# The forgetting heads' bias taken as the row of running sums, in four causal strips per head

## The chip, the cores and the metric

One core of one Trainium2 chip runs the whole program. The metric is device time in microseconds (us), the median of the runs shown. The engines are named as in the profile: PE (TensorE, the matrix engine; PEld is its loading of weights), DVE (VectorE), ACT (ScalarE), POOL (GpSimd) and SP (SyncE, which here only issues transfers). Each engine works through its own instructions strictly in order.

## The reference, cut to what matters

The program is one decoder layer on a sequence of 512 positions with width 1024: a feed-forward half step, a mixing step with two branches of attention, and a second feed-forward half step. The change lies in branch A, the forgetting attention, with 8 heads of 64:

```python
cum = jnp.cumsum(log_f, axis=1).transpose(0, 2, 1)
for start in range(0, S, Q_BLOCK):            # blocks of 128 queries
    end = start + Q_BLOCK
    logits = jnp.einsum('bqhd,bkhd->bhqk', q[:, start:end], k[:, :end]) * scale
    logits = logits + cum[:, :, start:end, None] - cum[:, :, None, :end]
    logits = jnp.where(kpos <= qpos, logits, NEG_INF)
    p = jax.nn.softmax(logits, axis=-1)
    outs.append(jnp.einsum('bhqk,bkhd->bqhd', p, v[:, :end]))
```

The first summand of the bias, `cum` at the query, is one number for a whole row of the softmax, and a softmax does not change when a constant is added to its row. The second, `cum` at the key, differs from column to column. Branch B, the sparse attention, has 8 more heads with a bias by distance and a selection of the 128 best keys.

## The kernel before, in words

Matmuls are made in three passes of a split number (high times high, low times high, high times low; lines 155 to 157). The feed-forward steps come first and last. Between them, from about 350 to 650 us, lie the projections and the 16 heads of attention: heads 0 to 7 are the forgetting ones, 8 to 15 the sparse ones. The order of PE is written out by hand: each head has four steps s = 0 to 3, and step s computes the scores of query block i = 3 - s (`ps_qk`, line 929 its last matmul) against n = 128 (i + 1) keys. Between the steps stand pieces of the projections, by a table of amounts (`FILL`), which keep PE busy while the other engines make the softmax. On PE the scores of one head are followed a head later by the transposes of its probabilities (`pt`, line 1251) and, one step after these, by the products with the values (`po`, lines 1261 and 1262).

In this stretch the order on DVE, ACT, POOL and SP is set when the program is built, by a scheduler that places each instruction where it expects its inputs to be ready; on the chip the order is fixed. The names that matter:

- `softmax_block` (lines 1233 to 1245). DVE adds bias and scores and takes the minimum of the row (scores stand there with reversed sign; line 1240, `p<-ps_qk,b`, called the score sum below), ACT takes the exponential (`p<-p,mn`, 1242), DVE the reciprocal of the row's sum (`rs`, 1243), and POOL multiplies by it (`p<-p,rs`, 1244).
- `flip` copies the transposed probabilities into a high part on ACT (`ph`, 1255) and a low part on DVE (`pl`, 1256).
- `get_bias(g)` (1306) loads, one head ahead, for a forgetting head the 512 running sums of that head into all 128 partitions (`cb`, 256 KB, from `cum_rows` in DRAM). Then for each of the four blocks POOL makes a tile `b`: it adds the negative running sum of the query (`ncum`, line 1314), and writes the large number BIG above the diagonal into the last 128 columns (line 1315).
- `forget` (1147) makes the running sums `cum` in the stretch before the heads, and from them `ncum` on DVE (line 1176), and writes `cum_rows`.
- Other work of POOL here: the inverse root for the norm of queries and keys (`rh`, 900), that norm's product (`kn`, 1004), and the sum of two halves of a head's result (`o`, 1272). Other work of DVE: the low parts of the weights (`wl`, 150), of the heads' results (`oAl`, 1276), of keys (`kl`, 890) and queries (`st`, 920), and until about 456 us the selection of keys for branch B (`m` and `sc`, 1189 to 1194).
- SP issues the loads of weights (line 143, three buffers `ra`, `rb`, `rc` in turn), the bias loads (1308) and copies of key halves (1302), in one queue.

Of the kernel before, what the change touches and what calls it, by code (L numbers as in the profile page):

```python
# [12 lines left out]
F32 = mybir.dt.float32  # L13
F32R = mybir.dt.float32r
AF = mybir.ActivationFunctionType
OP = mybir.AluOpType
# [3 lines left out]
P = 128  # L20
T = 512
NT = T // P
# [14 lines left out]
H = 8  # L37
# [3 lines left out]
BIG = 1e30  # L41
S_W = 208
# [13 lines left out]
def tile_hybrid_layer(ctx: ExitStack, tc: tile.TileContext, a: dict):  # L56
    nc = tc.nc
# [727 lines left out]
    with tc.tile_pool(name="begin", bufs=1) as bp, tc.manual_schedule(  # L785
# [40 lines left out]
        for nm in ("w_gate1", "w_up1"):  # L826
            tag = next(raw_tags)
# [41 lines left out]
    with (tc.tile_pool(name="mix", bufs=1) as mp, ExitStack() as att_ctx,  # L869
# [3 lines left out]
        rt = rb = None  # L873
        tn, fv, iq, pA, ga, gb = {}, {}, [], [], [], []
        kept = mp_dram.tile([P, 5, T], F32, name="kept")
        sg = at.tile([P, NT, S_W - 128], F32, name="sg")
        sd = [at.tile([P, NT, 2, DH], F32, tag="cb", bufs=2, name="sd") for _ in range(2)]
        dkh = at.tile([P, T], F32R, name="dkh")
        dkl = at.tile([P, T], F32R, name="dkl")
        dvv = at.tile([P, NT, P], F32R, name="dvv")  # L880
        cum = at.tile([P, NT, H], F32, name="cum")
        ncum = at.tile([P, NT, H], F32, name="ncum")
        dram = att_ctx.enter_context(tc.tile_pool(name="dram", bufs=1, space=bass.MemoryType.DRAM))
        cum_rows = dram.tile([H, T], F32, name="cum_rows")
        wi = at.tile([P, NT, H], F32, name="wi")
# [261 lines left out]
        def forget():  # L1147

            z = small.tile([P, NT, H], F32, tag="z", bufs=1, name="z")
            V.tensor_add(z, sg[:, :, 64:72], bf[:, None, :].to_broadcast([P, NT, H]))  # L1150
            na = small.tile([P, NT, H], F32, tag="na", bufs=1, name="na")
            V.scalar_tensor_tensor(na, z, -1.0, z, op0=OP.mult, op1=OP.min)
            e = small.tile([P, NT, H], F32, tag="e", bufs=1, name="e")
            S.activation(e, na, AF.Exp)
            u1 = small.tile([P, NT, H], F32, tag="u1", bufs=1, name="u1")
            V.tensor_scalar(u1, e, 1.0, None, op0=OP.add)
            ln = small.tile([P, NT, H], F32, tag="ln", bufs=1, name="ln")
            S.activation(ln, u1, AF.Ln)
            cr = small.tile([P, NT, H], F32, tag="cr", bufs=1, name="cr")
            V.tensor_scalar(cr, u1, 1.0, None, op0=OP.subtract)  # L1160
            V.tensor_sub(cr, e, cr)
            V.reciprocal(u1, u1)
            V.tensor_mul(cr, cr, u1)
            V.tensor_add(ln, ln, cr)
            lf = small.tile([P, NT, H], F32, tag="lf", bufs=1, name="lf")
            V.scalar_tensor_tensor(lf, z, 0.0, ln, op0=OP.min, op1=OP.subtract)
            before = small.tile([P, NT, H], F32, tag="u1", bufs=1, name="before")
            G.memset(before[:, 0], 0.0)
            for t in range(1, NT):
                V.tensor_add(before[:, t], before[:, t - 1], lf[:, t - 1])  # L1170
            yield
            pc = psum.tile([P, T], F32, tag="pt", bufs=2, name="pc")
            PE.matmul(pc[:, :NT * H], trin, lf.rearrange("p t h -> p (t h)"), start=True, stop=False)
            PE.matmul(pc[:, :NT * H], ones, before.rearrange("p t h -> p (t h)"), start=False, stop=True)
            V.tensor_copy(cum, pc[:, :NT * H].rearrange("p (t h) -> p t h", t=NT))
            V.tensor_scalar(ncum, cum, -1.0, None, op0=OP.mult)
            yield
            ps = psum.tile([P, T], F32, tag="pt", bufs=2, name="ps_ct")
            for t in range(NT):
                PE.transpose(ps[0:H, t * P:(t + 1) * P], cum[:, t], ident)  # L1180
            cum_t = tmp_tile("cum_t")[0:H]
            S.copy(cum_t, ps[0:H])
            nc.sync.dma_start(cum_rows, cum_t)
# [104 lines left out]
        def get_k(g):  # L1288
# [14 lines left out]
                out.append(k)  # L1303
            return out

        def get_bias(g):
            cb = at.tile([P, T], F32, tag="cb", bufs=2, name="cb")
            nc.sync.dma_start(cb, cum_rows[g:g + 1, :].to_broadcast([P, T]) if g < H else a["rel"][g - H])

            def bias(i):  # L1310
                n = P * (i + 1)
                b = tmp_tile("b")
                if g < H:
                    G.tensor_scalar(b[:, :n], cb[:, :n], 1.0, ncum[:, i, g:g + 1], op0=OP.mult, op1=OP.add)
                    G.affine_select(out=b[:, i * P:n], in_=b[:, i * P:n], compare_op=OP.is_ge, fill=BIG, base=0,
                                    pattern=[[-1, P]], channel_multiplier=1)
                else:
                    G.tensor_sub(b[:, :n], sc[i] if i else cpos, cb[:, T - n:T])
                return b[:, :n]
            return bias  # L1320

# [5 lines left out]
        for step in range(30):  # L1327
# [6 lines left out]
            if step == 15:  # L1334
                nq = get_q(0)
            if step == 24:
                nb = get_bias(0)
        prod.finish(upto["fv0"])


# [33 lines left out]
            return upto["dq1"] if g < 6 else upto["ga7"] if 4 * g + s < 4 * 9 + 2 else len(units)  # L1374

        for g in range(2 * H):
            q, k, bias = nq, nk, nb
            probs[g] = [None] * NT
            st = [small.tile([P, NT], F32, tag=nm, name=nm) for nm in ("mn", "rs")]
            for s in range(NT):  # L1380
# [4 lines left out]
                softmax_block(g, NT - 1 - s, q, k, bias, probs[g], st)  # L1385
                prod.run(FILL[g] / 2, limit(g, s))
                if g + 1 < 2 * H:
                    if s == 0:
                        nb = get_bias(g + 1)
                    if s == 0 and g % 2:  # L1390
                        nk = get_k(g + 1)
                    if s == 1 and g % 2:
                        nq = get_q(g + 1)
# [131 lines left out]
```

## Time and profile before

| | |
|---|---|
| median of 3 runs | 1044.01 us (1043.91 to 1044.5) |
| the profiled execution | 1043.44 us, its span 1041.7 us |
| PE busy in the span | 1027.9 us (99%) |
| DVE, ACT, POOL busy | 851.7, 668.8, 256.6 us |
| the forgetting heads' stretch, 420 to 532 us: PE, DVE, ACT, POOL busy | 105.35, 92.87, 78.35, 78.13 of 112 us |
| granted clock of PE | 1.00 throughout |

The page's parts follow each other: busy times, the span in 40 slices, transfers by queue, the chain of work that ended last, the costliest groups of instructions, and the transfers. The span is the time from the first to the last instruction that was profiled; the time of an execution contains about 2 us around it. In a row of a timeline the first number is the start in us from the span's start, the second the duration; a bracket gives the idle time of the engine before it and what ended it. PE's matmuls overlap, so that its busy time contains no gap that is shorter than one of them.

### The profile page before, as it was taken

The page shows a single profiled execution, that of the slowest core. Times are in us where ns is not written, and L with a number is a line of the kernel's source. Part 1 is how long each engine was busy: PE and PEld are TensorE (multiplying, and loading weights), DVE is VectorE, ACT ScalarE, POOL GpSimd, SP SyncE. Part 2 cuts the span into 40 slices and gives each one's busy share as a digit, 9 for nine tenths or more (in the row PEclk, how much of TensorE's full clock was granted, in tenths as well). Part 3 has the DMA queues.
Part 4 walks back from the last instruction along what each step waited for, and adds up shares of the span by engine and source line. Part 5 has one row for each costly group of instructions (what it writes and reads, how often), then busy time and mean ns, then how long its engine had stood idle before and what let it go on. Part 6 is the DMA issues. An engine that isn't in the chain of part 4 may idle for free.

```text
span 1041.7 us, 19489 instructions
## 1 busy us (share of the span) xinstructions
PE 1027.9 (99%) x7424; PEld 960.6 (92%) x7424; DVE 851.7 (82%) x1405; ACT 668.8 (64%) x1118; POOL 256.6 (25%) x324
## 2 busy tenths in 40 slices
PE   9999999999999999999999999999999999999998
PEld 8889999999999999989887788888889999999998
DVE  6897888897989779977868765853987888988887
ACT  6547765865787765567767665433736865875783
POOL 1100111120121124285867552000100210111111
PEclk9999999999999999999999999999999999999999
DMA  7444755666567367633314311532553665567554
GB/s 257 108 152 120 158 161 132 150 163 175 124 142 185 113 166 190 182 97 93 86 57 132 119 54 52 181 112 81 131 164 96 146 150 177 129 162 192 131 128 132
DMA packets 57341, 142.66 MB, mean 137 GB/s; under 512 B 6424, under 2 KB 15768, under 8 KB 57248
## 3 DMA queue, kind: packets, MB, share of 16 engines
q1 hardware_dynamic: 39600, 110.21, 34.1%
q0 software_dynamic: 17504, 30.94, 16.6%
q8 instruction: 58, 0.95, 0.4%
q10 hardware_dynamic: 144, 0.27, 0.1%
q14 instruction: 35, 0.29, 0.1%
HBM read 104.94 MB, written 3.42 MB: 104 GB/s over the span
## 4 chain that ended last, share of the span: by engine, by line
PE 89%; DVE 5%; POOL 3%; issue 2%; DMA 1%; ACT 1%; POOLq 0%; DVEq 0%; ACTq 0%
PE pB L155 5%; PE pB L157 5%; PE pB L156 5%; PE ps_f L155 3%; PE pA L155 3%; PE pA L157 3%; PE pA L156 3%; PE ps_f L157 3%; PE ps_f L156 3%; PE dB L157 2%; PE dB L155 2%; PE dB L156 2%; PE ps_t L157 2%; PE ps_t L155 2%; PE ps_t L156 2%; PE dA L156 2%
## 5 line engine op out<-in xcount | busy, mean ns | idle before, releaser
L123 ACT CAST wh<-s 128x1024 fp32r<-128x1024 f32 (+1 forms) x90 | 86.8, 965 | 66.8 <-PE pC L156 31.5
L130 DVE TENSOR_TENSOR wl<-s,wh 128x1024 fp32r<-128x1024 f32 (+1 forms) x90 | 100.4, 1116 | 19.9 <-ACT wh L123 19.9
L155 PE MATMUL ps_t<-wh,xh 128*128 128x256 f32 (+1 forms) x288 | 81.2, 282 | 0.0
L157 PE MATMUL ps_t<-wh,xl 128*128 128x256 f32 (+1 forms) x288 | 80.4, 279 | 0.0
L156 PE MATMUL ps_t<-wl,xh 128*128 128x256 f32 (+1 forms) x288 | 80.3, 279 | 0.0
L155 PE MATMUL pB<-tbh,wh 128*128 128x256 f32 x288 | 79.5, 276 | 0.0
L156 PE MATMUL pB<-tbl,wh 128*128 128x256 f32 x288 | 79.5, 276 | 0.0
L157 PE MATMUL pB<-tbh,wl 128*128 128x256 f32 x288 | 79.5, 276 | 0.0
L249 POOL DMA_DIRECT2D b<-gu x12 | 10.4, 864 | 220.3 <-DVE rb L449 89.4
L155 PE MATMUL ps_f<-xh,wh 128*128 128x512 f32 (+1 forms) x152 | 59.0, 388 | 0.0
L157 PE MATMUL ps_f<-xh,wl 128*128 128x512 f32 (+1 forms) x152 | 57.9, 381 | 0.0
L156 PE MATMUL ps_f<-xl,wh 128*128 128x512 f32 (+1 forms) x152 | 57.7, 380 | 0.0
L1242 ACT ACTIVATE p<-p,mn 128x512 f32<-128x512 f32 (+1 forms) x64 | 36.1, 564 | 29.5 <-DVE mn L1240 29.2
L155 PEld LDWEIGHTS ps_t<-wh,xh 128*128 128x128 f32 x288 | 54.5, 189 | 0.5
L156 PEld LDWEIGHTS ps_t<-wl,xh 128*128 128x128 f32 x288 | 54.4, 189 | 0.5
L157 PEld LDWEIGHTS ps_t<-wh,xl 128*128 128x128 f32 x288 | 54.4, 189 | 0.2 <-DVE xl L168 0.2
L157 PEld LDWEIGHTS pB<-tbh,wl 128*128 128x128 f32 x288 | 54.1, 188 | 0.0
L156 PEld LDWEIGHTS pB<-tbl,wh 128*128 128x128 f32 x288 | 54.1, 188 | 0.0
L155 PEld LDWEIGHTS pB<-tbh,wh 128*128 128x128 f32 x288 | 54.1, 188 | 0.0
L1244 POOL TENSOR_SCALAR p<-p,rs 128x512 f32<-128x512 f32 (+1 forms) x64 | 39.2, 615 | 58.9 <-DVE rs L1243 53.5
L575 POOL DMA_DIRECT2D gx<-e x20 | 23.9, 1241 | 119.4 <-ACT wh L123 99.9
L1256 DVE TENSOR_TENSOR pl<-pt,ph 128x512 fp32r<-128x512 f32 (+1 forms) x64 | 31.0, 485 | 17.7 <-ACT ph L1255 17.5
(406 smaller groups left out, 4195.9 us busy)
## 6 DMA issues: line engine op xcount, KB each, us to landing
rf<-in_w_pair_dram SPq DMA_DIRECT2D x15, 512.0 KB, 4.1
rc<-in_w_pair_dram SPq DMA_DIRECT2D x12, 512.0 KB, 3.6
re<-in_w_pair_dram SPq DMA_DIRECT2D x12, 512.0 KB, 3.6
rd<-in_w_pair_dram SPq DMA_DIRECT2D x12, 512.0 KB, 4.0
rb<-in_w_pair_dram SPq DMA_DIRECT2D x12, 512.0 KB, 4.3
gx<-e POOLq DMA_DIRECT2D x22, 256.0 KB, 4.3
ra<-in_w_pair_dram SPq DMA_DIRECT2D x9, 512.0 KB, 3.8
rd<-in_w_halves_dram SPq DMA_DIRECT2D x12, 384.0 KB, 3.7
```

Source lines behind the costliest of these rows:

```text
L123: S.copy(wh[:, :f], raw[:, :f])
L130: V.tensor_sub(wl[:, :f], raw[:, :f], wh[:, :f].bitcast(F32))
L155: PE.matmul(out, lh, rh, start=start, stop=False, **more)
L156: PE.matmul(out, lh, rl, start=False, stop=False, **more)
L157: PE.matmul(out, ll, rh, start=False, stop=stop, **more)
L249: G.dma_start(l, src, accum_op=OP.add)
L575: G.dma_start(xa[:, d:d + 2, HT:], t["e"][part], accum_op=OP.add)
L1242: S.activation(p, p, AF.Exp, bias=mn, scale=-1.0, accum_out=rs)
L1244: G.tensor_scalar(p, p, rs, 1.0, op0=OP.mult, op1=OP.mult)
L1256: V.tensor_sub(pl[:, sl], pt[:, sl], ph[:, sl].bitcast(F32))
```

## The change

The running sum of the query is no longer added. The bias of block i is then the same in all rows of the block except for the diagonal, and is loaded for each block by itself into all 128 partitions, as a strip of n = 128 (i + 1) columns. POOL writes BIG above the diagonal into the strip in place, and DVE's score sum reads the strip. So each forgetting head has four loads (256, 192, 128 and 64 KB) in place of one of 256 KB, and four instructions on POOL (the diagonal) in place of eight; `ncum` is no longer made.

The strips of blocks 3 and 2 use the two buffers of `cb`, those of blocks 1 and 0 share one buffer, which held `sg` before. Strip 3 of the next head is asked for after the second step of a head, strip 2 after its third step, and strips 1 and 0 after the first step of their own head. A load can start when the score sum that read its buffer has ended. In PE's order nothing moves.

```diff
-        sg = at.tile([P, NT, S_W - 128], F32, name="sg")
+        sg = at.tile([P, 3 * P], F32, tag="sg", name="sg")[:, :NT * (S_W - 128)].rearrange("p (t c) -> p t c", t=NT)
...
+            cum = small.tile([P, NT, H], F32, tag="cr", bufs=1, name="cum")
             V.tensor_copy(cum, pc[:, :NT * H].rearrange("p (t h) -> p t h", t=NT))
-            V.tensor_scalar(ncum, cum, -1.0, None, op0=OP.mult)
...
+        def causal_rows(g, i):
+            if i:
+                strip = at.tile([P, T] if i > 1 else [P, 3 * P], F32, tag="cb" if i > 1 else "sg",
+                                bufs=2 if i > 1 else 1, name="cb")
+            else:
+                strip = strips[1][:, 2 * P:]
+            n = P * (i + 1)
+            nc.sync.dma_start(strip[:, :n], cum_rows[g:g + 1, :n].to_broadcast([P, n]))
+            G.affine_select(out=strip[:, i * P:n], in_=strip[:, i * P:n], compare_op=OP.is_ge, fill=BIG, base=0,
+                            pattern=[[-1, P]], channel_multiplier=1)
+            strips[i] = strip
+
+        def forget_bias(i):
+            return strips[i][:, :P * (i + 1)]
...
-            nc.sync.dma_start(cb, cum_rows[g:g + 1, :].to_broadcast([P, T]) if g < H else a["rel"][g - H])
+            nc.sync.dma_start(cb, a["rel"][g - H])
...
-                if g < H:
-                    G.tensor_scalar(b[:, :n], cb[:, :n], 1.0, ncum[:, i, g:g + 1], op0=OP.mult, op1=OP.add)
-                    G.affine_select(out=b[:, i * P:n], in_=b[:, i * P:n], compare_op=OP.is_ge, fill=BIG, base=0,
-                                    pattern=[[-1, P]], channel_multiplier=1)
-                else:
-                    G.tensor_sub(b[:, :n], sc[i] if i else cpos, cb[:, T - n:T])
+                G.tensor_sub(b[:, :n], sc[i] if i else cpos, cb[:, T - n:T])
...
             if step == 24:
-                nb = get_bias(0)
+                for i in (3, 2, 1, 0):
+                    causal_rows(0, i)
...
-            q, k, bias = nq, nk, nb
+            q, k, bias = nq, nk, forget_bias if g < H else nb
...
                 if g + 1 < 2 * H:
-                    if s == 0:
+                    if s and g + 1 < H:
+                        for i in ((), (3,), (2,), ())[s]:
+                            causal_rows(g + 1, i)
+                    if s == 0 and g + 1 >= H:
                         nb = get_bias(g + 1)
+                    if s == 0 and 0 < g < H:
+                        for i in (1, 0):
+                            causal_rows(g, i)
```

The scheduler's order on the other engines moves with it. The prediction speaks of three places. The first is POOL between the scores of head 1 and the last probabilities of head 2 (`p<-p,rs` with 512, 384, 256 and 128 columns is one head). Before:

```order
L1244 TENSOR_SCALAR p<-p,rs 128x512
L1004 TENSOR_TENSOR kn<-kn,rh 128x512
L1272 TENSOR_TENSOR o<-o_5868,o 64x512
L1315 AFFINE_SELECT b<-b 128x128
L1314 TENSOR_SCALAR b<-cb,ncum 128x256
L1314 TENSOR_SCALAR b<-cb,ncum 128x128
L1314 TENSOR_SCALAR b<-cb,ncum 128x512
L1315 AFFINE_SELECT b<-b 128x128
L900 TENSOR_TENSOR rh<-ss,nhalf 128x8
L1315 AFFINE_SELECT b<-b 128x128 x2
L1244 TENSOR_SCALAR p<-p,rs 128x384
```

And now:

```order
L1242 TENSOR_SCALAR p<-p,rs 128x512
L898 TENSOR_TENSOR rh<-ss,nhalf 128x8
L1312 AFFINE_SELECT cb<-cb 128x128
L1270 TENSOR_TENSOR o<-o_5870,o 64x512
L1002 TENSOR_TENSOR kn<-kn,rh 128x512
L1242 TENSOR_SCALAR p<-p,rs 128x384
```

Three additions and three diagonals between the first two multiplications are gone; the diagonals that are left belong to the head after.

The second place is POOL at the multiplications of heads 1 and 5. Before, around those of head 1:

```order
L1244 TENSOR_SCALAR p<-p,rs 128x384
L1244 TENSOR_SCALAR p<-p,rs 128x256
L1314 TENSOR_SCALAR b<-cb,ncum 128x512
L1244 TENSOR_SCALAR p<-p,rs 128x128
L1315 AFFINE_SELECT b<-b 128x128
```

And now:

```order
L1312 AFFINE_SELECT cb<-cb 128x128
L1242 TENSOR_SCALAR p<-p,rs 128x256
L1312 AFFINE_SELECT cb<-cb 128x128
L1242 TENSOR_SCALAR p<-p,rs 128x128
L1242 TENSOR_SCALAR p<-p,rs 128x512
```

The two diagonals here are those of strips 1 and 0 of head 2, and both now stand ahead of the last multiplication of head 1. Those of head 6 stand in the same way ahead of the last one of head 5, and those of head 1 ahead of the last one of head 0.

The third place is DVE at the end of the selection for branch B, between the last score sum of head 1 (128 columns) and the low parts of the transposes of head 0. Before:

```order
L150 TENSOR_TENSOR wl<-rc,wh 128x1024
L1240 ISA p,mn<-ps_qk,b 128x128
L1240 ISA mn 128x1
L1243 RECIPROCAL rs<-rs 128x1
L1256 TENSOR_TENSOR pl<-pt,ph 128x256
L1194 TENSOR_SCALAR sc_4155<-sc_4155 128x512
```

And now:

```order
L1238 ISA p,mn<-ps_qk,cb 128x128
L1238 ISA mn 128x1
L150 TENSOR_TENSOR wl<-rc,wh 128x1024
L1192 TENSOR_SCALAR sc_4153<-sc_4153 128x512
L1241 RECIPROCAL rs<-rs 128x1
L1254 TENSOR_TENSOR pl<-pt,ph 128x256
```

The score sum moved ahead of the weights' low part, and the selection's last step (`sc`, 512 columns) moved ahead of `pl`.

More of the change, by code (lines that the diff above doesn't have):

```diff
@@ L880, in tile_hybrid_layer @@
         dvv = at.tile([P, NT, P], F32R, name="dvv")
-        cum = at.tile([P, NT, H], F32, name="cum")
-        ncum = at.tile([P, NT, H], F32, name="ncum")
         dram = att_ctx.enter_context(tc.tile_pool(name="dram", bufs=1, space=bass.MemoryType.DRAM))
@@ L1304, in get_k @@
             return out
+        def causal_rows(g, i):
[9 more added lines that the diff above has]
+            strips[i] = strip
+        strips = {}
+        def forget_bias(i):
+            return strips[i][:, :P * (i + 1)]
         def get_bias(g):
             cb = at.tile([P, T], F32, tag="cb", bufs=2, name="cb")
-            nc.sync.dma_start(cb, cum_rows[g:g + 1, :].to_broadcast([P, T]) if g < H else a["rel"][g - H])
+            nc.sync.dma_start(cb, a["rel"][g - H])
             def bias(i):
```

## The prediction

> **What bounds the kernel now.** I began with the first part of the page and the chain of waits. (Rows: the span, busy time by engine, the chain's shares.)
>
> ```profile
> span 1041.7 us, 19489 instructions
> PE 1027.9 (99%) x7424; PEld 960.6 (92%) x7424; DVE 851.7 (82%) x1405; ACT 668.8 (64%) x1118; POOL 256.6 (25%) x324
> PE 89%; DVE 5%; POOL 3%; issue 2%; DMA 1%; ACT 1%; POOLq 0%; DVEq 0%; ACTq 0%
> ```
>
> PE bounds the program as a whole, and an edit that leaves PE's work alone can win only what PE waits. The chain leaves PE for a tenth of the time, so the next view is the busy time in stretches, around the forgetting heads, and then what PE waits for there (columns: total, times, longest).
>
> ```profile
> core 0: us, PE busy (x) PEld busy (x) DVE busy (x) ACT busy (x) POOL busy (x), PEclk, DMA share, GB/s
> 380.00:427.00 47.00, 47.00 (x339) 43.78 (x338) 46.78 (x134) 25.44 (x36) 20.07 (x20) 1.00 0.74 185
> 427.00:445.00 18.00, 17.29 (x145) 16.91 (x144) 17.97 (x55) 13.17 (x26) 7.95 (x17) 1.00 0.44 143
> 420.00:532.00 112.00, 105.35 (x805) 99.66 (x804) 92.87 (x231) 78.35 (x169) 78.13 (x117) 1.00 0.36 105
> ```
>
> ```profile
> PE pt L1251 <- POOL p L1244: 2.4, 3, 1.4
> PE pt L1251 <- DVE pl L1256: 1.9, 2, 1.1
> PE po L1262 <- DVE pl L1256: 1.4, 2, 0.8
> PE pt L1251 <- DVE rs L1243: 0.6, 1, 0.6
> ```
>
> In the 112 us of the forgetting heads PE is idle 6.65 us, of which these four rows hold 6.3. So the ceiling of the change is about 6.65 us, 0.6%. Two regimes share it. Up to about 456 us DVE is the bound (46.78 of 47 us busy, then 17.97 of 18), through the selection for branch B; afterwards POOL and DVE hold each other up.
>
> **What is removed: 32 additions on POOL.** (A tile's row: shortest, median, longest; then rows of timelines of DVE, POOL and PE.)
>
> ```profile
> L1314 POOL TENSOR_SCALAR b<-cb,ncum x32: 368/539/1543, 425.3 to 527.0; 128x512 f32<-128x512 f32 x8, 128x384 f32<-128x384 f32 x8, 128x256 f32<-128x256 f32 x8, 128x128 f32<-128x128 f32 x8
> 464.82 1.95 POOL L1314 TENSOR_SCALAR b<-cb,ncum 128x256 f32<-128x256 f32 x3
> 468.94 0.29 DVE L1240 CUSTOM_DVE_ANT_0 p<-ps_qk,b 128x128 f32<-128x128 f32 x1 [0.62 <-POOL b L1315]
> 470.15 1.04 POOL L1004 TENSOR_TENSOR kn<-kn,rh 128x512 f32<-128x512 f32 x1
> 469.87 2.42 DVE L150 TENSOR_TENSOR wl<-rb,wh 128x1024 fp32r<-128x1024 f32 x1
> 473.08 0.66 PE L1251 MATMUL pt<-ident,p 128*128 128x128 f32 x4 [1.43 <-POOL p L1244]
> 505.85 0.28 PE L155 MATMUL ps_t<-wh,xh 128*128 128x256 f32 x1
> 505.97 0.28 PE L156 MATMUL ps_t<-wl,xh 128*128 128x256 f32 x1
> ```
>
> At the median 32 x 0.54 = 17 us go from POOL's 78.13. They matter where PE waits. A matmul here lasts 0.28 us but the next starts 0.12 us later, so each wait costs 0.16 us more than its idle.
>
> At 473.08 PE stands for 1.43 us. Its probabilities wait for the sum that stands at 468.94, which had waited for its bias behind the three additions from 464.82 on; then `wl` (2.42 us) keeps the reciprocal from being made. Three additions (1.95 us) are gone from this place, as the first pair of orders shows, and the bias now lies ready a step before. With 1.95 us against 1.43 + 0.16 I take the whole: **-1.6**.
>
> ```profile
> 501.46 0.56 DVE L1240 CUSTOM_DVE_ANT_0 p<-ps_qk,b 128x384 f32<-128x384 f32 x1 [0.26 <-POOL b L1315]
> 504.68 0.41 PE L1251 MATMUL pt<-ident,p 128*128 128x128 f32 x2 [0.62 <-DVE rs L1243]
> 517.21 2.57 DVE L1276 TENSOR_TENSOR oAl<-o,oAh 64x512 fp32r<-64x512 f32 x1
> 518.75 1.60 POOL L1314 TENSOR_SCALAR b<-cb,ncum 128x128 f32<-128x128 f32 x2
> 520.23 0.39 PE L1262 MATMUL po<-pl,fv 128*128 128x256 f32 x1 [0.78 <-DVE pl L1256]
> 521.20 0.27 DVE L1240 CUSTOM_DVE_ANT_0 p<-ps_qk,b 128x128 f32<-128x128 f32 x1
> 523.36 0.33 PE L1251 MATMUL pt<-ident,p 128*128 128x128 f32 x1 [0.23 <-POOL p L1244]
> ```
>
> Three smaller waits are shared. At 504.68 DVE lost only 0.26 us to the bias, so I take 0.26 + 0.16 = **-0.4** of 0.62 + 0.16. At 520.23 `oAl` held DVE for 2.57 us, the end of it beside two additions (1.60); I take half of 0.78 + 0.16, **-0.5**, since the additions cover only the last part. At 523.36 the probabilities come from the score sum of 521.20, which is behind that same block: all of 0.23 + 0.16, **-0.4**.
>
> **What is removed on DVE: `ncum`.**
>
> ```profile
> 407.28 1.46 DVE L1176 TENSOR_SCALAR ncum<-cum 128x32 f32<-128x32 f32 x1
> 407.32 1.37 POOL L1004 TENSOR_TENSOR kn<-kn,rh 128x512 f32<-128x512 f32 x1
> 411.37 0.15 DVE L898 TENSOR_SCALAR ss<-ss 128x8 f32<-128x8 f32 x1
> 455.84 0.39 PE L1262 MATMUL po<-pl,fv 128*128 128x256 f32 x1 [0.66 <-DVE pl L1256]
> 455.70 0.62 DVE L1194 TENSOR_SCALAR sc<-sc 128x512 f32<-128x512 f32 x1
> ```
>
> Thirty-two columns took 1.46 us, as long as POOL's product beside it (a small one of the kind takes 0.15). DVE has no slack from there to 456, so all of it comes earlier behind this place by 1.46 us, if nothing else is held in its stead (then 0). I take **-1.3**, near the upper end, because the instructions around it are of the selection, which no row shows held. Against it stands the third place of the order: the selection's last step (0.62) now goes ahead of the `pl` for which PE waits at 455.84: **+0.6**.
>
> **What is added: 24 transfers, and POOL's waiting for them.**
>
> ```profile
> DMA to landing us min/median/max: 3.1/3.6/5.9
> L1308 SPq DMA_DIRECT2D cb<-cum_rows x8: 319/342/540, 420.6 to 501.2; - x8
> 506.33 0.29 DVE L1240 CUSTOM_DVE_ANT_0 p<-ps_qk,b 128x128 f32<-128x128 f32 x1
> 502.32 0.29 POOL L1315 TENSOR_SCALAR_AFFINE_SELECT b<-b 128x128 f32<-128x128 f32 x1
> 455.09 0.29 DVE L1240 CUSTOM_DVE_ANT_0 p<-ps_qk,b 128x128 f32<-128x128 f32 x1
> 522.94 0.37 POOL L1244 TENSOR_SCALAR p<-p,rs 128x128 f32<-128x128 f32 x1
> 510.14 0.60 PE L1251 MATMUL pt<-ident,p 128*128 128x128 f32 x4
> 458.65 0.49 PE L1251 MATMUL pt<-ident,p 128*128 128x128 f32 x3
> SPq L143 <- DVE wl L150: 30.9, 5, 8.0
> ```
>
> The first row is of the tile of running sums, the last of SP's own waits. At three places (the second pair of orders) a multiplication stands behind diagonals whose strips may be loaded only after the last score sum of the same head. For head 5: the sum ends at 506.33 + 0.29, two issues follow (0.34 each, the second strip starts its way after the first issue), 3.6 to land, a diagonal 0.29, a multiplication 0.37, which is 511.2. PE needs it at 510.14, so 1.1 late; with the sum up to 0.6 earlier, since no bias holds it, 0.5. I take **+0.8**. For head 1 the sum ended at 455.09 + 0.29; less the 1.3 from above that is 454.1, and 458.7 by the same steps, which is just PE's 458.65: 0, since the sum has also moved ahead of a `wl`. For head 0 the same wait lies under DVE's lag: 0. Bounds: landing in 3.1 makes head 5 wait 0 to 0.6; landing in 5.9 makes it 3.1, and head 1 up to 2.4.
>
> By the Trainium skill, DMA: Bandwidth & Descriptors, "Anatomy of one DMA", a transfer costs about 2.0 us and its bytes at 436 GB/s (fitted for transfers issued by POOL), here 2.3 us for 128 KB. The trace has 3.1 at the least for 256 KB. By the page the term of 0.8 would be 0 and the sum 0.8 lower.
>
> SP issues 24 more transfers, at 0.34 some 8 us in 112, and 640 in place of 256 KB per head, 3 MB or 27 GB/s on top of 105, below the 185 of the stretch before. The weights behind them in the queue are covered: SP stands 30.9 us waiting for their buffers, in five waits of up to 8.0, and no row of PE's waits names a weight. Cost 0; without that cover 0.34 per strip ahead of a load. The diagonals stay (32 as before), PE's rows stay, and the tile pools give nothing that a wait shows.
>
> **The sum.** -1.6 - 0.4 - 0.5 - 0.4 - 1.3 + 0.6 + 0.8 = -2.8 us. The profiled execution took 1043.44 (span 1041.7), 0.57 under the median of 1044.01; 1040.6 there is 1041.2 for the median, -0.27%.
>
> **The rivals.** *The blocks move instead of going.* The `wl` of 2.42 us at 469.87 stood beside the product `kn` (470.15), which is not removed, and `oAl` began before the additions did. If DVE's two-operand instructions are held by whichever POOL instruction runs, a lighter POOL meets them elsewhere and only the bias waits go. Of the five gains 0.4 and 0.4 and half of 1.6 stay, of 1.3 nothing: -1.6 + 0.6 + 0.8 = -0.2, 1043.8. For it speaks that in these 112 us the additions are about a fifth of POOL's work (17 of 78); against it that both waits stood behind additions.
>
> The Trainium skill, SBUF — State Buffer, "SBUF: two separate sides", says that DVE and GpSimd take a shared pair of ports as an exclusive lock for a whole instruction. The 1.46 beside 1.37 agrees; by that rule the time held follows from what meets, not from POOL's load, which is this rival.
>
> *Late strips, slower.* Place: POOL's queue, where a diagonal that waits for its strip keeps the multiplications behind it. At a landing of 5.9 it costs 3.1 + 2.4 = 5.5 in place of 0.8; with the gains of the forecast that is -2.8 + 4.7 = +1.9, 1045.9, and with those of the first rival +4.5, 1048.5. It turns slower from a landing of about 5.0 in the one case (1.4 us more at both heads) and of 3.8 in the other. For it: the transfers more than double. Against: the DMA share there is 0.36, half of what the stretch before bore.
>
> *All waits go.* With POOL at four fifths of its load and DVE ahead, the whole 6.65 vanishes, and 0.16 for each of the eight waits that the rows count, less 0.8: -7.1, 1036.9. Against it: the DVE-bound waits have DVE's work as their cause, which stays.
>
> **Numbers.** Forecast 0.55, blocks move 0.24, late strips 0.12, all go 0.09. What this measurement can tell from no change is 0.2%, 2.1 us. Of the forecast 0.50 lies beyond that line and 0.05 within it, of the first rival 0.01 and 0.23; with the others that makes faster 0.60, same 0.28, slower 0.12. The forecast's own bounds are its terms at their ends: -1.6 - 0.4 - 0.9 - 0.4 - 1.5 with nothing added is -4.8 (1039.2); without the gains at 520 and of `ncum`, and with 0.6 and 1.1 added, it is -0.7 (1043.3). The range goes on past half the way from the forecast to "all go" (1038.4) and over the first rival into the beginning of the second, 1044.4.
>
> **What would show it.** PE idle in 420 to 532 falls from 6.65 to about 4. Right: no wait of DVE's score sum for POOL, no PE wait of over 1 us behind POOL's `p` near 473, `cum` not followed by a held instruction, the last waits near 456 shorter. A multiplication of head 5 that waits for a transfer shows the +0.8. Wrong: `wl` or `oAl` of over 2 us again, new waits of PE on `p` or `pl` at heads 2 to 7, POOL waiting for `cb` by more than 1 us in several places, or PE waiting for weights.

## The result, and the profile after

The changed kernel takes 1052.93 us (median of 5 runs, 1052.47 to 1054.66) against 1044.01 beside it: ratio 1.0091, 95% interval 1.008 to 1.0103. It is slower by 0.9%, where 1041.2 was forecast. Its profiled execution took 1053.75 us with a span of 1052.0, 10.3 us more than the span of before.

The first part of the page and the chain of waits, after:

```profile
span 1052.0 us, 19502 instructions
PE 1033.3 (98%) x7424; PEld 966.0 (92%) x7424; DVE 849.4 (81%) x1404; ACT 668.8 (64%) x1118; POOL 239.8 (23%) x292
PE 94%; DVE 3%; DMA 1%; issue 1%; ACT 0%; POOL 0%; SPq 0%; DVEq 0%; POOLq 0%
```

POOL lost 16.8 us of work and 32 instructions, as the change says. PE has the same 7424 matmuls, yet its busy time rose by 5.4 us: matmuls became longer. The chain alone would mislead, since it lies on PE even more than before and says nothing of their speed.

The stretches that the prediction used, after (columns as there; PEclk is the third number from the end):

```profile
380.00:427.00 47.00, 47.00 (x338) 43.80 (x338) 46.78 (x139) 25.43 (x36) 19.28 (x19) 1.00 0.74 173
427.00:445.00 18.00, 15.04 (x113) 14.57 (x112) 13.22 (x40) 8.26 (x17) 4.05 (x8) 0.91 0.61 174
420.00:532.00 112.00, 99.85 (x752) 95.86 (x752) 84.34 (x213) 70.35 (x153) 52.94 (x77) 0.95 0.45 125
```

Up to 427 the busy times are as before. From there PE stands 12.15 us where it stood 6.65, DVE is idle where it had no slack (13.22 of 18 us, before 17.97), and the granted clock is 0.91 and 0.95. The waits in the 112 us (total, times, longest):

```profile
POOL cb L1312 <- DMA cb<-cum_rows: 44.3, 18, 10.3
ACT wh L144 <- DMA rc<-in_w_fq_dram: 8.3, 1, 8.3
PE pt L1249 <- POOL p L1242: 7.2, 3, 3.4
PE ps_qk L926 <- DVE mn L1238: 3.0, 1, 3.0
PE pt L1249 <- DVE pl L1254: 1.9, 3, 0.8
```

Three long waits of PE have come: 2.96, 3.38 and 3.40 us. Of the short ones less than half is left in all (counted below). Each long wait has a timeline.

**The first, at 438.95.** (Rows of SP, ACT, DVE and PE.)

```profile
421.59 0.82 SPq L1311 DMA_DIRECT2D cb<-cum_rows  x2
422.93 0.95 SPq L1311 DMA_DIRECT2D cb<-cum_rows  x2
423.99 0.43 SPq L143 DMA_DIRECT2D rc<-in_w_fq_dram  x1
433.81 1.05 ACT L144 CAST wh<-rc 128x1024 fp32r<-128x1024 f32 x1 [8.32 <-DMA rc<-in_w_fq_dram]
434.89 1.23 DVE L150 TENSOR_TENSOR wl<-rc,wh 128x1024 fp32r<-128x1024 f32 x1 [4.75 <-ACT wh L144]
438.33 0.55 DVE L1238 CUSTOM_DVE_ANT_0 p<-ps_qk,cb 128x384 f32<-128x384 f32 x1
438.95 0.33 PE L926 MATMUL ps_qk<-kh,st 128*128 128x128 f32 x1 [2.96 <-DVE mn L1238]
```

All four strips of head 0 stand ahead of the weights `rc`, which arrive 9.7 us after their issue (before: issued at 421.05, arrived 5.5 us later). ACT's cast waits 8.32 us, DVE's `wl` 4.75 us behind it, the score sum of head 0's second block stands behind `wl`, and PE's next score waits for the PSUM buffer which that sum empties.

**The second, at 450.16, and the third, at 520.92.** (DVE's last score sum of heads 0 and 5, SP's issue of the next head's last strips, for head 0 DVE's last reciprocal, then POOL's diagonals, the multiplication, PE.)

```profile
443.38 0.28 DVE L1238 CUSTOM_DVE_ANT_0 p<-ps_qk,cb 128x128 f32<-128x128 f32 x1
443.69 1.98 SPq L1311 DMA_DIRECT2D cb<-cum_rows  x3
446.69 0.15 DVE L1241 RECIPROCAL rs<-rs 128x1 f32<-128x1 f32 x1
447.69 2.06 POOL L1312 TENSOR_SCALAR_AFFINE_SELECT cb<-cb 128x128 f32<-128x128 f32 x2 [2.98 <-DMA cb<-cum_rows]
449.74 0.37 POOL L1242 TENSOR_SCALAR p<-p,rs 128x128 f32<-128x128 f32 x1
450.16 1.11 PE L1249 MATMUL pt<-ident,p 128*128 128x128 f32 x4 [3.38 <-POOL p L1242]
...
514.64 0.28 DVE L1238 CUSTOM_DVE_ANT_0 p<-ps_qk,cb 128x128 f32<-128x128 f32 x1
514.99 0.80 SPq L1311 DMA_DIRECT2D cb<-cum_rows  x2
518.71 0.29 POOL L1312 TENSOR_SCALAR_AFFINE_SELECT cb<-cb 128x128 f32<-128x128 f32 x1 [3.87 <-DMA cb<-cum_rows]
520.22 0.29 POOL L1312 TENSOR_SCALAR_AFFINE_SELECT cb<-cb 128x128 f32<-128x128 f32 x1 [1.21 <-DMA cb<-cum_rows]
520.49 1.04 POOL L1242 TENSOR_SCALAR p<-p,rs 128x128 f32<-128x128 f32 x2
520.92 0.66 PE L1249 MATMUL pt<-ident,p 128*128 128x128 f32 x4 [3.40 <-POOL p L1242]
```

This is the mechanism of the second rival: the load starts only when the last score sum has freed the single buffer of the last strips, and the multiplication that PE waits for stands in POOL's queue behind the diagonals. At head 0 the reciprocal was ready at 446.84, and the multiplication began 2.9 us later.

**The clock after each.** Stretches of 3.41 us, each pair being one that ends where the granted clock falls, and the one that follows (first number: length, second: PE busy):

```profile
436.53:439.94 3.41, 0.99 (x8) 0.99 (x9) 3.41 (x12) 3.10 (x7) 1.00 (x2) 1.00 0.47 161
439.94:443.35 3.41, 3.41 (x16) 3.29 (x15) 3.41 (x10) 1.96 (x5) 1.09 (x1) 0.50 0.18 58
...
446.77:450.18 3.41, 0.03 (x2) 0.02 (x1) 3.41 (x11) 2.21 (x6) 2.49 (x4) 1.00 0.58 171
450.18:453.59 3.41, 3.41 (x15) 3.41 (x16) 1.64 (x6) 1.27 (x2) 3.33 (x4) 0.50 0.44 159
...
518.45:521.86 3.41, 0.94 (x8) 0.94 (x9) 0.00 (x0) 0.24 (x2) 1.86 (x5) 1.00 0.58 161
521.86:525.27 3.41, 3.41 (x17) 3.41 (x16) 2.82 (x5) 2.70 (x6) 1.20 (x1) 0.50 0.26 49
```

For 3.41 us after each wait PE runs at half its clock, which costs 1.7 us more each time. Before, no such stretch lay inside the program.

The account, by the starts of the matmuls (a wait is the step from one start to the next, less the usual 0.11 us): the three waits cost 3.13 + 3.55 + 3.57 = 10.25 us and the half clock 3 x 1.7 = 5.1; the short waits in 420 to 532 (each over 0.2 us) fell from 8.6 to 3.8 in all, which gives back 4.8. That is +10.5 against the 10.3 by which the span grew.

### The profile page after: what moved, and what is told of

It is laid out like the page before. It is cut to its first block, busy times and chain, and to the rows that moved or that the text cites. A ratio compares the mean times of both kernels' runs of the same rounds, so it can differ in the third digit from the quotient of the medians.

```text
span 1052.0 us, 19502 instructions
## 1 busy us (share of the span) xinstructions
PE 1033.3 (98%) x7424; PEld 966.0 (92%) x7424; DVE 849.4 (81%) x1404; ACT 668.8 (64%) x1118; POOL 239.8 (23%) x292
## 4 chain that ended last, share of the span: by engine, by line
PE 94%; DVE 3%; DMA 1%; issue 1%; ACT 0%; POOL 0%; SPq 0%; DVEq 0%; POOLq 0%
PE pB L155 5%; PE pB L156 5%; PE pB L157 5%; PE ps_f L155 3%; PE ps_f L157 3%; PE ps_f L156 3%; PE pA L155 3%; PE pA L156 3%; PE pA L157 3%; PE ps_t L155 3%; PE ps_t L157 3%; PE ps_t L156 3%; PE dB L157 2%; PE dB L155 2%; PE dB L156 2%; PE dA L156 2%
```

## The experiments

Ratios are to the kernel before, beside which each was run (its median there was 1043.0 to 1043.8), with 95% intervals.

**Head 0's strips apart.**

```diff
             if step == 24:
-                for i in (3, 2, 1, 0):
-                    causal_rows(0, i)
+                causal_rows(0, 3)
+            if step == 27:
+                causal_rows(0, 2)
...
-                    if s == 0 and 0 < g < H:
+                    if s == 0 and g < H:
                         for i in (1, 0):
                             causal_rows(g, i)
```

> The changed kernel with one thing moved: of head 0's four strips only the first is loaded where all four stood; the second comes a pass later, and the last two after the first pass of head 0, as at the other heads. So one strip and not four stands in SP's queue ahead of the weights rc of the forget branch. Theory queue (the wait of 2.96 us at 438.95 comes from the weights, which landed behind four strips that came about 2 us apart, and the half clock of 3.41 us from 439.94 follows from that wait): both go. 2.96 + 0.16 + 3.41/2 = -4.8 us against the changed kernel, about 1048.1, still slower than before. Rival bytes (the strips' traffic as such, wherever it is issued, slows the weights): the wait stays within 1 us of 2.96, 1052 to 1053. Rival POOL (head 0's diagonals on POOL delay the score sums, whatever the weights do): the wait becomes one on the last multiplication of head 0, as at head 5, of 2 us or more: 1051 to 1053.

Measured: 1048.91 us, ratio 1.0056 (1.0041 to 1.0071). The wait at 438.95 is gone and no other has come in its place; against the change's 1.0091 that is -3.7 us of the -4.8 expected. The waits of heads 0 and 5 stay (3.15 and 3.46 us). So the place of the four strips ahead of the weights was the cause; whether their number or their bytes, this run does not tell.

**Buffers that are free.**

```diff
-                strip = at.tile([P, T] if i > 1 else [P, 3 * P], F32, tag="cb" if i > 1 else "sg",
-                                bufs=2 if i > 1 else 1, name="cb")
+                strip = at.tile([P, T], F32, tag="cb", bufs=2, name="cb") if i > 1 else tmp_tile("cb")
```

> The changed kernel with one thing changed: the strips of rows 1 and 0 are put into the six buffers of 512 columns in which the bias stood before the change, and no longer into one buffer of their own. Their loads then need not wait for the last score sum of the head before; nothing else moves in the program's text, and head 0's four strips stay ahead of the weights. Theory release (the waits of 3.38 us at 450.16 and 3.4 us at 520.92 come from loads that cannot start until the single buffer is free, with POOL's multiplication behind the diagonals): both go with the half clock behind each. 2 x (3.4 + 0.16 + 1.7) = -10.5 us at the most, about 1042.5; the wait at 438.95 stays. Rival order (the loads would come as late, because SP issues them after the same score sums for other reasons): the waits stay, 1052 to 1053. Rival small waits (the places then meet the waits that stood there before the change, 0.5 to 1.4 us): 1044 to 1046.

Measured: 1048.34 us, ratio 1.0046 (1.0031 to 1.006): by the ratios 4.7 us less than the change. The wait at 520.92 is gone with its half clock. That of head 0 only fell, from 3.38 to 2.18 us at 446.09, and it still brought a half clock; with the weights in time as well it is 1.19 us (next run), so the late weights fed it. The strips hold the multiplication at neither place any more: at head 0 it now waits 1.42 us for DVE's reciprocal. So the release theory holds, and its -10.5 was too much, because at head 0 DVE's lag behind the late weights lay under the wait for the strips. (The profiled execution took 1045.45 us, the others 1048.07 to 1048.73; in it the first wait, at 437.67, was 1.86 us and brought no half clock.)

**Both.**

> Both edits: head 0's strips spread over the passes, and the last two strips of a head in the six free buffers. If the three long waits with their half clock are the whole loss and nothing else in the change costs more than it gives, all 15.3 us (10.25 of waits by the starts of matmuls, 5.1 of half clock) go: 1037.7, faster than before by 0.6%, a little more than the sum of the prediction's gains (-3.6 without its 0.8). If the transfers as such cost something beside these waits (24 more issues on SP, 640 in place of 256 KB a head), it ends between 1040 and 1045. If the waits only move to the next late thing, above 1045.

Measured: 1043.11 us, ratio 0.9997 (0.9988 to 1.0006). With both causes out, all three long waits and all half clock are gone, and with them the whole loss. But the change gives nothing either: it stays 5.4 us above the 1037.7 expected, in the range that was put down to the transfers as such, which the runs on transfers below test. PE's waits are now short ones. Rows of this kernel around 456, 464 and 519 (PE, DVE, POOL):

```profile
456.88 0.39 PE L1260 MATMUL po<-pl,fv 128*128 128x256 f32 x1 [0.99 <-DVE pl L1254]
455.16 1.27 DVE L1192 TENSOR_SCALAR sc<-sc 128x512 f32<-128x512 f32 x1
460.96 0.56 DVE L1238 CUSTOM_DVE_ANT_0 p<-ps_qk,cb 128x384 f32<-128x384 f32 x1 [1.27 <-POOL cb L1311]
463.66 3.29 DVE L150 TENSOR_TENSOR wl<-ra,wh 128x1024 fp32r<-128x1024 f32 x1 [0.77 <-ACT wh L144]
463.58 1.28 POOL L1270 TENSOR_TENSOR o<-o,o 64x512 f32<-64x512 f32 x1
464.83 1.04 POOL L1002 TENSOR_TENSOR kn<-kn,rh 128x512 f32<-128x512 f32 x1
465.85 1.55 POOL L1242 TENSOR_SCALAR p<-p,rs 128x384 f32<-128x384 f32 x1
518.61 2.35 DVE L1274 TENSOR_TENSOR oAl<-o,oAh 64x512 fp32r<-64x512 f32 x1
```

The selection's last step, ahead of `pl`, takes 1.27 us and PE waits 0.99; a score sum waits 1.27 us for a diagonal; `wl` takes 3.29 us beside `o`, `kn` and a multiplication, where 1.22 is its usual time, and that multiplication takes 1.55 where 0.59 is usual; `oAl` takes 2.35 us where 0.68 is usual. The Trainium skill, SBUF — State Buffer, "SBUF: two separate sides", has a DVE instruction with two inputs in SBUF and a GpSimd instruction that reads SBUF lock each other out of a shared pair of ports for whole instructions; the 3.29 beside these three agrees. In 420 to 545 the 15 `wl` and 7 `oAl` take 27.8 us before and 28.0 here: with 32 additions fewer on POOL, DVE is held as long. So the blocks had moved, as the first rival said, in this kernel.

**PE kept busy in two of the waits.**

```diff
             pt = psum.tile([P, T], F32, tag="pt", bufs=2, name="pt")
+            for _ in range(12 if j == 0 and pr in (probs[0], probs.get(5)) else 0):
+                PE.matmul(pt[:, 0:P], ones, ones, start=True, stop=True)
             for i in range(j, NT):
```

> The changed kernel with 24 matmuls of 128x128 more on TensorE that change no result: 12 each into the PSUM tile of the transposes, ahead of the transposes of the last probabilities of heads 0 and 5, for which PE stands at 450.16 and 520.92. They fill part of these two waits and remove none of their causes. Theory clock (a PE wait of over 3 us is followed by 3.41 us at half the granted clock, and it is the idle that does it): both half-clock stretches go while the last probabilities come as late as before: -2 x 1.7 = -3.4 us, about 1049.5, and the third stretch, at 439.94, stays. Rival (the half clock has another cause, such as the load of the transfers or a time that only happens to fall there): the stretches stay, and the time is the same or up to 24 x 0.1 = 2.4 us longer where the added matmuls overrun a wait.

Measured: 1049.62 us, ratio 1.0064 (1.0047 to 1.008), 2.8 us under the change (-3.4 expected; each added matmul is two instructions in the trace, 24 in 2.84 us at head 0). In its profiled execution only the stretch behind the first wait, from 439.34, is at half clock. Nothing about strips, POOL or transfers was changed, and the half clock behind the two filled waits is gone, so it is due to PE's idling.

**`ncum` taken out by subtracting.**

```diff
-            V.tensor_scalar(ncum, cum, -1.0, None, op0=OP.mult)
...
-                    G.tensor_scalar(b[:, :n], cb[:, :n], 1.0, ncum[:, i, g:g + 1], op0=OP.mult, op1=OP.add)
+                    G.tensor_scalar(b[:, :n], cb[:, :n], 1.0, cum[:, i, g:g + 1], op0=OP.mult, op1=OP.subtract)
```

> The kernel before with one part of the change alone: POOL's additions subtract cum instead of adding ncum, so that the operation that made ncum (1.46 us on DVE at 407.28) is gone and all the rest stays. Theory of the prediction (DVE is the bound from there to 456, so this time comes off): -1.3 us, about 1041.7. Rival blocks (the time was POOL's product kn holding whatever DVE had to do there; the next instruction is held in its place): 0, within 0.5 us of before. Rival other waits (in DVE's stretch the end is set by PE's order of work, which absorbs it): also 0.

Measured: 1068.23 us, ratio 1.0248 (1.0235 to 1.0261): 25 us slower, outside every expectation. The groups of POOL in 420 to 532, of before and then of this kernel (count | busy, mean ns | idle before):

```profile
L1314 POOL TENSOR_SCALAR b<-cb,ncum 128x512 f32<-128x512 f32 x8 | 6.7, 841 | 10.1 <-DMA cb<-cum_rows 10.1
```

```profile
L1312 POOL TENSOR_SCALAR b<-cb,cum 128x512 f32<-128x512 f32 x7 | 14.2, 2030 | 11.1 <-DMA cb<-cum_rows 11.1
```

On POOL the same operation with subtract for add takes 2.03 us in place of 0.84. So the run says nothing of `ncum`, which a later run tests in another way.

**One row, no additions, no transfers added.** Taken from the kernel before:

```diff
-            V.tensor_scalar(ncum, cum, -1.0, None, op0=OP.mult)
...
-                b = tmp_tile("b")
                 if g < H:
-                    G.tensor_scalar(b[:, :n], cb[:, :n], 1.0, ncum[:, i, g:g + 1], op0=OP.mult, op1=OP.add)
-                    G.affine_select(out=b[:, i * P:n], in_=b[:, i * P:n], compare_op=OP.is_ge, fill=BIG, base=0,
+                    G.affine_select(out=cb[:, i * P:n], in_=cb[:, i * P:n], compare_op=OP.is_ge, fill=BIG, base=0,
                                     pattern=[[-1, P]], channel_multiplier=1)
+                    return cb[:, :n]
```

> The kernel before with the 32 additions and ncum removed and no transfer added: each head loads its one row of running sums as before, and POOL writes the diagonal block of rows i into that row in place, right before the score sum of block i (the blocks go from 3 to 0, so a block is overwritten only after the longer ones have used it; rows below need it no more). Theory of the prediction (the short waits stood behind the additions and go with them): -1.6 - 0.4 - 0.5 - 0.4 - 1.3, up to -4.2 us, about 1038.8 to 1040. Rival blocks (DVE's wl and oAl are held by whichever instruction of POOL runs, and meet kn, o and the multiplications instead): at most the waits for a bias go, -1.6 to 0, 1041.4 to 1043. Rival chain (each select now has to wait for the score sum of the block before and each score sum for its select behind POOL's multiplications): slower than before by 1 to 4 us, with score sums waiting for POOL.

Measured: 1042.26 us, ratio 1.0001 (0.9991 to 1.0011), no difference. Three of its twelve executions, the profiled one among them (1045.4), took 1045.4 to 1046.8 us at a mean granted clock of 0.997, the others 1041.4 to 1043.3. Of the short waits less than half is left, but here too a select waits for its row on POOL (2.27 us before 442.71, 3.88 us before 513.92), with the last multiplications of heads 0 and 5 behind it. PE's rows:

```profile
444.67 1.12 PE L1249 MATMUL pt<-ident,p 128*128 128x128 f32 x4 [3.46 <-POOL p L1242]
514.62 0.66 PE L1249 MATMUL pt<-ident,p 128*128 128x128 f32 x4 [1.84 <-POOL p L1242]
```

The same trap as in the change, then, and set by buffers, not by strips: the row is held until the last score sum, and there are two.

**One row in free buffers.**

```diff
-            cb = at.tile([P, T], F32, tag="cb", bufs=2, name="cb")
+            cb = tmp_tile("cb") if g < H else at.tile([P, T], F32, tag="cb", bufs=2, name="cb")
```

> The one-row kernel of the run before with its row of running sums in the six free buffers, so that a row's load need not wait for the score sums of the head two before it. In that run POOL's select for a later head stood waiting for its row (2.27 us at 442.71, 3.88 us at 513.92) with the last multiplication of heads 0 and 5 behind it, and PE stood for 3.6 and 2.0 us, with 6.83 us at half clock in the profiled execution. Theory release: both waits go, and with them every half-clock stretch; against the undisturbed times of the one-row kernel (about 1042.1) -3.6 - 2.0 + two small waits of about 0.8 = -4, about 1038, faster than before by 0.4%. Rival (PE then meets DVE's lag at those places): the waits shrink to 1 to 1.5 us, 1040 to 1041.5. Rival: no difference, 1042.

Measured: 1039.52 us, ratio 0.9966 (0.9954 to 0.9979): faster than before by 0.34% and than the change by 1.2%. The wait of head 0 has shrunk to 0.91 us, that of head 5 is gone, no stretch is at half clock, and in 420 to 532 PE is busy 107.78 us (before 105.35). This version beats both kernels. It stays 1.5 us above the 1038 of the theory; PE's longest wait is now 1.43 us for DVE's `pl`, at 448.19.

**`ncum` made on another engine.**

```diff
-            V.tensor_scalar(ncum, cum, -1.0, None, op0=OP.mult)
+            S.mul(ncum, cum, -1.0)
```

> The kernel before with ncum made by ScalarE from cum, and all else as it was: the additions stay additions, unlike in the run that subtracted, where each took 2.4 times as long. This leaves the 1.46 us at 407.28 out of DVE's work. Theory of the prediction: -1.3 us, about 1041.7. Rival blocks (what DVE does instead beside POOL's kn is held as long): 0, 1042.5 to 1043.5. Rival other waits: the gain at 407 is used up by 456 in waits for other work: 0 too, but with DVE idle in that stretch.

Measured: 1041.68 us, ratio 0.9985 (0.9976 to 0.9994), -1.5 us. So the size of the term of -1.3 was right, its place only in part: set beside the same matmuls of before, those of this trace gain 0.6 us between 430 and 457, where DVE's stretch ends, and 1.0 more by 485. There PE's wait near 473, by the starts, falls from 1.59 to 0.76 us although the additions stay, so in this kernel the term and the -1.6 are not separate.

**What do the transfers cost?** Between the kernel with both edits (0.9997) and the one-row kernel in free buffers (0.9966) lie 3.2 us. Three runs change the latter's transfers alone.

```diff
-            nc.sync.dma_start(cb, cum_rows[g:g + 1, :].to_broadcast([P, T]) if g < H else a["rel"][g - H])
+            for t in range(NT if g < H else 0):
+                c = slice(t * P, t * P + P)
+                nc.sync.dma_start(cb[:, c], cum_rows[g:g + 1, c].to_broadcast([P, P]))
+            if g >= H:
+                nc.sync.dma_start(cb, a["rel"][g - H])
```

> The one-row kernel with free buffers (1039.5), with each head's row loaded by four transfers of 128 columns in place of one of 512: 24 issues more on SP, as in the change, and not a byte more. Head 0's four stand ahead of the weights rc of the forget branch. Theory queue (each of these transfers holds the ones behind it by about 2 us whatever its size): rc lands some 6 us later and the wait of 3 us of PE before head 0's last score comes back, with half clock behind it in part of the executions: +3 to +5, 1042.5 to 1044.5. Rival bytes (what made the weights late was 640 KB, not the number of transfers): no more than the issues themselves, 3 x 0.33 = 1 us at this place, most of it hidden: 1039.5 to 1040.5.

> The same, but head 0's row is one transfer; only heads 1 to 7 have four. This leaves 21 more issues and takes the place ahead of the weights rc away. It is to tell where the 3.6 us lie by which the kernel with both edits (1043.1) stays behind the one-row kernel with free buffers (1039.5). Theory transfers (24 more of them cost what they cost in SP's queue, wherever they stand): 2 to 3.6 us of the 3.6 here, 1041.5 to 1043. Rival POOL (the cost of the strips is that POOL's selects stand waiting, one after the other, each for a strip of its own that is loaded only just before it, with products and multiplications behind them): here the row is loaded as early as before, so 0 to 0.7, 1039.5 to 1040.2.

```diff
             nc.sync.dma_start(cb, cum_rows[g:g + 1, :].to_broadcast([P, T]) if g < H else a["rel"][g - H])
+            if 0 < g < H:
+                nc.sync.dma_start(tmp_tile("idle"), cum_rows[g:g + 1, :].to_broadcast([P, T]))
```

> The one-row kernel with free buffers (1039.5), in which heads 1 to 7 load their row a second time, right behind the first, into a buffer that nobody reads: 512 KB per head in place of 256, against 640 with the strips. The order of the other engines is the same to the last instruction. Theory bytes (the 3.6 us by which the kernel with both edits stays behind this one are the strips' added traffic of 384 KB a head, which makes weights and rows late): two thirds of it are added here, so about +2, 1041.5 or more. Rival POOL (the cost lies in selects that wait on POOL, each for a strip that is loaded just before it): the row that is read lands as early as before, +0 to +0.5, 1039.5 to 1040.

Measured, in this order: 1040.69 us, 0.9974 (0.9962 to 0.9985); 1039.57 us, 0.9963 (0.9951 to 0.9976); 1039.93 us, 0.9966 (0.9954 to 0.9978). Neither 21 more transfers nor 256 KB more for each of seven heads costs anything that shows. With head 0's row in four pieces ahead of the weights, the time is 0.8 us more by the ratios, about what the rival gave for the issues alone; PE's wait at head 0 is 1.79 us in place of 0.91, and no longer one comes. The issue rows of the weights in 420 to 436, of before, of the change and of the run in pieces (KB, median us to landing):

```profile
rc<-in_w_fq_dram SPq DMA_DIRECT2D x1, 512.0 KB, 5.5
```

```profile
rc<-in_w_fq_dram SPq DMA_DIRECT2D x1, 512.0 KB, 9.7
```

```profile
rc<-in_w_fq_dram SPq DMA_DIRECT2D x1, 512.0 KB, 5.6
```

The change and the run in pieces both put four transfers of `cb` ahead of these weights, and issue the weights at 423.99 and 424.56. In the change the four carry 640 KB, here 256, and the weights take 9.7 and 5.6 us. So the long wait came from the bytes ahead of them, not from the number; my theory of 2 us for each transfer falls.

What is left for the 3.2 us is what the traces show: POOL's rows of waits for `cb` in 420 to 545, of the kernel with both edits and of the one-row kernel in free buffers.

```profile
POOL cb L1311 <- DMA cb<-cum_rows: 33.4, 15, 11.3
```

```profile
POOL cb L1311 <- DMA cb<-cum_rows: 16.5, 3, 11.5
```

Fifteen selects wait for a strip of their own in the one and three in the other, and POOL's products come at other times beside DVE's work. Set side by side, the same matmuls of the two traces part at three places, by 1.0, 1.1 and 1.1 us. They are those of the rows above: around 456 the selection's last step stands ahead of `pl` in the one and behind it in the other; around 464 there are the score sum that waits for its diagonal and the `wl` of 3.29 us, here 2.26; around 519 the `oAl` of 2.35, here 0.68. In all, `wl` and `oAl` take 28.0 us with both edits and 24.9 here. So the traces show where the 3.2 us arise. That the selects' waiting for strips is behind all of it is argued, and not shown by a run of its own; the order at 456 is the scheduler's.

**PE kept busy in the one-row kernel.** The same matmuls, in the kernel with two buffers. (The executions at 0.997 were three of twelve, not four as written below.)

> The one-row kernel with the two waits of 3.6 and 2.0 us (two buffers only), and the same 24 matmuls that change no result ahead of the last transposes of heads 0 and 5. Without them 4 of 12 executions took 1045.4 to 1046.8 at a mean granted clock of 0.997 and the rest 1041.4 to 1043.3 at 1.0. Theory window (the clock is halved when a PE idle stretch fills enough of one interval of 3.41 us of a grid that doesn't start with the program, so that it hits some executions of the same kernel and not others): with the idle filled, every execution has clock 1.0 and lies between 1041.4 and 1043.5. Rival (the disturbed executions have another cause): a third of them stays at 0.997 and above 1045.

Measured: 1043.84 us, ratio 1.0007 (0.9999 to 1.0016). All 11 executions lie between 1043.53 and 1044.08 with a clock of 0.999 or 1.0, and none at 0.997. The spread is gone, as the theory of the window has it. But all lie just above its range: the added matmuls cost 1.7 us against the 1042.1 of the executions that had kept their clock, so this is no way to win.

## Why the prediction was wrong

- **"The weights behind them in the queue are covered", cost 0.** This step failed first. I read the cover from SP's five waits for weight buffers, and priced a strip ahead of a load at its issue, 0.34 us. The price was in the bytes: 384 KB more ahead of one 512 KB load made it land after 9.7 us in place of 5.5 (and it was issued 2.9 us later than before, a delay that the run in pieces bore as well, without the long wait), at a place where DVE had no slack and the next score sum stood behind that weight's `wl`. Measured: 3.13 us, and the half clock.
- **"For head 0 the same wait lies under DVE's lag: 0."** The lag hid little of it: DVE's reciprocal was ready at 446.84, and the multiplication stood behind the diagonals until 449.74, 2.9 us more. Measured: 3.55 us of wait. With the weights in time and the buffer still bound (first experiment) the wait is 3.15 us all the same, so the step was wrong in its own right.
- **Head 5, +0.8.** The mechanism was right and the size wrong: 3.4 us of idle. From the end of the sum (514.92) to PE took 6.0 us, where I had 4.6: the two strips landed 3.6 and 4.8 us after their issue, and the second diagonal came 1.5 us behind the first. PE was ready 2.6 us after the sum, where I took 3.5 from before, and the sum was not 0.6 earlier. The upper bound of 3.1, from a landing of 5.9, was close. The figure of the Trainium skill (DMA: Bandwidth & Descriptors, "Anatomy of one DMA"), fitted for transfers issued by POOL, would have made this term 0; the trace speaks against it.
- **The clock.** No step held it: a third of the loss (5.1 of 15.3 us) is matmuls at half clock behind the three waits. I priced a wait at its own length plus 0.16.
- **-1.6, -0.4, -0.5, -0.4 and -1.3.** Of these 4.2 us the one-row kernel in free buffers gains 3.5 (0.34%), and `ncum` alone 1.5 where I had 1.3. If the two add up, which no run tests, 2.0 is left for the additions, where I had 2.9. In the change they also show: over the wait at 473 its matmuls gain 1.6 us on those of before, as forecast, and the short waits are 4.8 us less in all, though part of that came free: behind a long wait of PE everything else is ahead.
- **+0.6 for the selection's last step ahead of `pl`.** Right in kind: with both edits it takes 1.27 us there and PE waits 0.99. In the change PE's wait at that `pl` was 0.38 by the starts.
- **The rivals.** "Late strips, slower", at a chance of 0.12, had the place and the mechanism of two of the three waits, at a price without the clock and without the weights. "The blocks move instead of going" is what the kernel shows once the strips are in time (0.9997, `wl` and `oAl` 28.0 us in place of 27.8); with a row in free buffers part of them does go (24.9). What would have told: the row order on SP, where four strips come ahead of `rc`, in a stretch whose DMA share was 0.74 just before, and the single buffer for the last two strips.

## What to carry to other kernels

Before a load is split or doubled, find what stands behind it in its queue and what stands behind that on the engine that waits: bytes put ahead of one late weight cost more here than 21 transfers put elsewhere. Where a buffer is freed by the last use of a step and an in-order queue holds its refill's consumer ahead of work that the bottleneck needs, a second buffer is worth more than the work that was saved: it decided between 1.0001 and 0.9966. And a wait of TensorE of some 2 us or more can bring a half clock behind it, 1.7 us here, and has to be priced with it.

## What the runs showed of the hardware

**The half clock follows a grid.** In the change it set in at 439.94, 450.18 and 521.86, the latter two 3 and 24 intervals of 3.413 us after the first. Whether it sets in depends on how busy PE was in one interval of that grid. Of the first experiment (wait 3.15 us, ended at 444.84) and of the second (wait 2.18 us, ended at 446.09), the interval with the end of the wait and the next:

```profile
442.98:446.39 3.41, 1.55 (x13) 1.55 (x14) 2.62 (x8) 1.74 (x5) 3.24 (x4) 1.00 0.64 211
446.39:449.80 3.41, 3.41 (x30) 3.33 (x29) 3.33 (x8) 2.20 (x5) 2.01 (x3) 1.00 0.45 129
```

```profile
443.13:446.54 3.41, 1.23 (x12) 1.03 (x10) 3.41 (x11) 3.25 (x7) 1.19 (x4) 1.00 0.70 243
446.54:449.95 3.41, 3.41 (x18) 3.41 (x16) 3.41 (x10) 1.27 (x2) 2.33 (x3) 0.50 0.40 123
```

The longer wait lay across two intervals, left PE busy for 1.55 us in the second, and cost no clock; the shorter lay within one, left 1.23, and did. With 1.41 us busy the one-row kernel was halved too. Over the 14 traces of this case, ten intervals at full clock within the program were followed by one at half clock, with PE busy for 0.00 to 1.41 us in them; none with 1.55 or more was. So the line lies somewhere between 1.41 and 1.55 of 3.41 us in these runs. A half clock can also last longer: in the one-row kernel PE was busy for 1.96 us of the interval at half clock, and the next was at half clock too. The Trainium skill, TensorE: Matmul & The Clock Gate, Part 1, describes a free-running window of 3413 ns, and the traces agree; the page's rule of no idle gaps over about 3 us ("Why this matters for your kernels") is too lenient for a wait of 2.18 us and too strict for one of 3.15.

**A subtraction on GpSimd.** `tensor_scalar` with multiply and subtract took 2.03 us on 128x512, with multiply and add 0.84; the mean over 128x128 was 0.71 us against 0.38.
